# Block products with shared sums for an FFN's down projection

## The chip, the cores and the metric

One core of one Trainium2 chip. The metric is the device time of one execution in microseconds; for the kernel before it is the median of three runs. A profile of one execution stands beside it.

## The reference

An encoder layer for 1024 tokens of width 1024, all in float32:

```python
x = layer_norm(a * x + 0.5 * swiglu(x, ffn1...), ln1...)
x = layer_norm(a * x + hybrid_mixer(x, ...), ln2...)
x = layer_norm(a * x + 0.5 * swiglu(x, ffn2...), ln3...)

def swiglu(x, w_gate, w_up, w_down):
    return (silu(x @ w_gate) * (x @ w_up)) @ w_down
```

`a` is 2^0.25, and the FFN width is 2816, that is 22 tiles of 128. The mixer is neighbourhood attention beside differential attention. The change touches only `@ w_down` of the two FFNs and what makes its operands.

## The kernel before, in words

TensorE multiplies in the type fp32r. To hold accuracy, every float32 operand is split in two: `hi`, a cast of the value on ACT (line 65), and `lo`, the value less `hi`, on DVE or POOL (line 66). A product is then three matmuls, hi x hi, hi x lo and lo x hi, summed in PSUM (`mm3`, lines 79 to 81). `split_w` (line 68) is load, cast and subtraction in one; its load goes through one of two staging buffers, `wst`.

Stages follow each other in time: gate/up of FFN1 (to about 430 us), its down product and normalisation (to about 715), the mixer, gate/up of FFN2 (1336 to 1762), its down product and the last normalisation.

**Gate/up** (`gate_up`, line 179) makes, for each of the 22 FFN tiles `f`, the 128 x 1024 tile h = 0.5 silu(gate) * up and stores it in DRAM (`hTd`, lines 195 to 210). Tiles 0 and 1 take plain products. Tiles 2 to 21 take a product of 2 x 2 blocks (gate and up by two halves of the model width; the same halves by two halves of the tokens) by seven block products in place of eight: sums of blocks of x are made once (`S2`, `S3`, `S4`), sums of blocks of the weights for each tile, in a tile `wr` of seven slots (`sums`, lines 238 to 240), and `splits` (line 245) then splits the seven. One turn of the loop at line 302 is seven products of 12 matmuls each. `wr` has one buffer: the load for the next tile (line 217) can start when the last split of this one has read it. `finish(f)` multiplies and stores. In the last turns `split_w` also fetches the first operands of the down product.

**Down** (`down_phase`, line 340) computes y[token block] += h[f] x w_down[f]. It walks over `CHUNKS`: eight pairs of FFN tiles, two single tiles, and a last chunk of four. For each chunk and each of eight token blocks `Rows.down` (line 114) sums the chunk's matmuls in a PSUM bank for either half of the 1024 columns, and DVE adds the bank to the float32 row block y in SBUF (line 127; the first chunk is copied by ACT, line 125). Operands of the chunk ahead are fetched by `split_w` with the subtraction on POOL. The residual is loaded into `xp` and added on the way (lines 356 to 363). In the last chunk each finished row block is normalised.

Engines run in order, each its own queue; all these DMAs are issued by SP (SyncE). The order within a queue is that of a planner, which takes instructions by their place in the program and by when it reckons their inputs to be there, and so moves them past each other: in the loop, the load for the next tile goes out ahead of the store of the tile before.

PSUM has eight banks: pool `psA` has two buffers of two banks, `psB` four of one.

Of the kernel before, what the change touches and what calls it, by code (L numbers as in the profile page):

```python
# [9 lines left out]
FT = mybir.dt.float32  # L10
FR = mybir.dt.float32r
# [3 lines left out]
OP = mybir.AluOpType  # L15
AX = mybir.AxisListType
TAIL = 3
# [3 lines left out]
P = 128  # L21
S = 1024
DM = 1024
# [21 lines left out]
def tile_hybrid_layer(ctx: ExitStack, tc: tile.TileContext, I: dict, out: bass.AP, dbg=None):  # L45
# [51 lines left out]
    hTd = [dr.tile([NF, P, S], FT, name=f"hTd{i}") for i in range(2)]  # L97
# [80 lines left out]

    def gate_up(n, wgu, wd, W0=None, prelude=None):


        with ExitStack() as es:
# [12 lines left out]
            def finish(f):  # L195
                h = wst.tile([P, 1024], FT, name="wst")
                V.scalar_tensor_tensor(h, u.rearrange("p t c -> p (t c)"), 0.5, sg.rearrange("p t c -> p (t c)"),
                                       OP.mult, OP.mult)
                dma(hTd[n][f], h)

            def plain(f, wt, ts):
                for t in ts:
                    h = tb_.tile([P, 512], FT, name="t")
                    ps = psA.tile([P, 2, 512], FT, name="psA")
                    for j in range(2):
                        mm3(ps[:, j], [wt(j, k) + xk(t, k) for k in range(KT)])
                        flush()
                    A.activation(sg[:, t], ps[:, 0], AF.Silu)
                    V.scalar_tensor_tensor(h, ps[:, 1], 0.5, sg[:, t], OP.mult, OP.mult)
                    dma(hTd[n][f, :, t * 512:(t + 1) * 512], h)  # L210
# [22 lines left out]
            def sums(f):  # L233
                l = L[f]
                o = wa.tile([P, 2, 512], FR, name="wa")
                split(o[:, 0], o[:, 1], l[:, 4], V)
                O[f, 4] = o[:, 0], o[:, 1]
                V.tensor_tensor(l[:, 0:4:3], l[:, 2:4], l[:, 3:5], OP.subtract)  # L238
                V.tensor_tensor(l[:, 5], l[:, 0], l[:, 4], OP.add)  # L239
                V.tensor_tensor(l[:, 6], l[:, 1], l[:, 5], OP.subtract)  # L240

            def splits(f, part):
                a, b = ((1, 5), (0, 3), (2, 6))[part]
                o = wb.tile([P, 2, 2, 512], FR, name="wb")
# [43 lines left out]
            wb = es.enter_context(tc.tile_pool(name=f"wb{n}", bufs=4))  # L288
            for i in range(3):
                splits(2, i)  # L290
            plain(1, at(1), (0,))

# [9 lines left out]
            for f in range(2, NF):  # L302
# [5 lines left out]
                prod(b, f, 1, A12)  # L308
                V.tensor_tensor(sg[:, 0], B[f, 1], b, OP.add)
# [5 lines left out]
                if more:  # L315
                    sums(f + 1)
                prod(a, f, 0, S3, False)
# [3 lines left out]
                if more:  # L321
                    splits(f + 1, 0)
                    first(f + 1)
                    splits(f + 1, 1)
                prod(a, f, 6, A22, False)
# [6 lines left out]

                k = f - (NF - 6)
                if 0 <= k < 4:
                    down0.append(split_w((hTd[n], wd)[k % 2][k // 2]))
        return down0

    CHUNKS = [(f, f + 1) for f in range(0, NF - 6, 2)] + [(NF - 6,), (NF - 5,), tuple(range(NF - 4, NF))]

    def down_phase(es, n, wd, down0, resid, g, b, post):  # L340

        m = Rows(es, n)
        hp = es.enter_context(tc.tile_pool(name=f"hp{n}", bufs=4))
        wp = es.enter_context(tc.tile_pool(name=f"wp{n}", bufs=4))
        xp = es.enter_context(tc.tile_pool(name=f"xp{n}", bufs=2))
        m.small(es, n)
        Hs, Ws = {0: down0[0], 1: down0[2]}, {0: down0[1], 1: down0[3]}

        def fetch(f):
            Hs[f] = split_w(hTd[n][f], *(() if f == NF - 1 else (hp, "hd")))  # L350
            Ws[f] = split_w(wd[f], *(() if f == NF - 1 else (wp, "wd")))

        def part(f):
            return lambda tb: (Hs[f][:, 0, tb * P:(tb + 1) * P], Hs[f][:, 1, tb * P:(tb + 1) * P])

        def residual(tb):
            x = xp.tile([P, DM], FT, name="xp")
            dma(x, resid(tb))

            def add():  # L360
                V.scalar_tensor_tensor(m.y[tb], x, ALPHA, m.y[tb], OP.mult, OP.add)
            return add

        for f in CHUNKS[1]:
            fetch(f)
        add = None
        for i, fs in enumerate(CHUNKS):
            last = i == len(CHUNKS) - 1
            ahead = [f for c in CHUNKS[i + 1:i + 2] if i for f in c]

            def each(tb):
                nonlocal add
                if 2 <= i < 6 and tb % 4 == 1:
                    add = residual(2 * (i - 2) + tb // 4)
                if add and tb % 4 == 3:
                    add()
                    add = None
                if tb % 2 == 0 and ahead:
                    fetch(ahead.pop(0))
                if i == 6 and tb == 7:  # L380
                    m.load_gb(g, b)

            m.down([part(f) for f in fs], [Ws[f] for f in fs], None if i == 0 else 1.0,
                   (lambda tb, st: post(m, tb, st)) if last else None, each)
            for f in ahead:
                fetch(f)
# [546 lines left out]
```

## Time and profile before

| | us |
|---|---|
| runs of the kernel before | 2022.59, 2018.19, 2023.49 |
| median | 2022.59 |
| profiled execution | 2018.42 |
| its span, first to last instruction | 2016.6 |
| TensorE busy | 1972.8 |
| DVE, ACT, POOL busy | 1168.2, 720.9, 424.2 |

PE is TensorE's matmuls, PEld its weight loads, DVE is VectorE, ACT ScalarE, POOL GpSimd, SP the engine that issues the DMAs. Busy times are shares of one execution and overlap; matmuls are pipelined, so a matmul's own duration is longer than the distance from one to the next. "Idle before" is the time in which an engine stood still ahead of the instruction, with what ended it behind the arrow. Lines such as L127 are those of the kernel.

### The profile page before, as it was taken

The numbers are of one execution on the slowest core, as the hardware profiler recorded it, in microseconds if no ns is written. First come the engines' busy times: TensorE is split into PE (matmuls) and PEld (weight loads), VectorE is DVE, ScalarE is ACT, GpSimd is POOL, SyncE is SP. The second block draws the span as 40 slices with busy tenths as digits, with TensorE's granted clock in tenths as the row PEclk, the third lists the DMA queues.
The fourth block names the chain that finished last, engine by engine and source line by source line (L and its number), as shares of the span: only waits on it lengthen the run. The fifth ranks groups of instructions, "written<-read, shape, count | busy, mean of one in ns | idle before, by whom it ended". The sixth has DMA issues, their size and how long they took to land. (4 is left out here: it accounts for less than half of the span.)

```text
span 2016.6 us, 24187 instructions
## 1 busy us (share of the span) xinstructions
PE 1972.8 (98%) x9368; PEld 1602.4 (79%) x9368; DVE 1168.2 (58%) x1803; ACT 720.9 (36%) x1206; POOL 424.2 (21%) x276
## 2 busy tenths in 40 slices
PE   9999999999999999999999999999999999999998
PEld 7788888887887778888777777888888788877877
DVE  8445455534657856777663345885545446336667
ACT  5233333332122245656544454123333333231121
POOL 0000000105345221111044443100000001044355
PEclk9999999999999999999999999999999999999999
DMA  4212212224323231112122226122221223144332
GB/s 163 79 73 94 84 74 105 98 95 156 124 98 132 91 108 40 37 50 61 29 55 65 62 74 230 63 84 78 79 84 74 94 70 119 64 167 145 106 104 84
DMA packets 51891, 186.05 MB, mean 92 GB/s; under 512 B 7360, under 2 KB 11328, under 8 KB 46400
## 3 DMA queue, kind: packets, MB, share of 16 engines
q1 hardware_dynamic: 51776, 184.50, 27.0%
q8 instruction: 74, 1.21, 0.3%
q14 instruction: 41, 0.34, 0.1%
HBM read 136.24 MB, written 39.85 MB: 87 GB/s over the span
## 5 line engine op out<-in xcount | busy, mean ns | idle before, releaser
L127 DVE SCALAR_TENSOR_TENSOR y<-y,psB 128x512 f32<-128x512 f32 (+1 forms) x358 | 238.8, 676 | 201.1 <-PE psB L81 197.2
L66 POOL TENSOR_TENSOR wsp<-wst,wsp 128x1024 fp32r<-128x1024 f32 x40 | 97.9, 2449 | 945.5 <-ACT wsp L65 945.5
L79 PE MATMUL psB<-wd,hd 128*128 128x512 f32 (+1 forms) x620 | 241.6, 390 | 5.4 <-DVE y L127 4.0
L80 PE MATMUL psB<-wd,hd 128*128 128x512 f32 (+1 forms) x620 | 240.5, 388 | 3.9 <-POOL wd L66 3.9
L81 PE MATMUL psB<-wd,hd 128*128 128x512 f32 (+1 forms) x620 | 240.2, 387 | 0.0
L79 PE MATMUL psA<-s,wb 128*128 128x512 f32 x480 | 189.7, 395 | 0.0
L81 PE MATMUL psA<-s,wb 128*128 128x512 f32 x480 | 187.2, 390 | 0.0
L80 PE MATMUL psA<-s,wb 128*128 128x512 f32 x480 | 186.8, 389 | 0.0
L66 DVE TENSOR_TENSOR wb<-wr,wb 128x1024 fp32r<-128x1024 f32 x120 | 157.0, 1317 | 47.3 <-ACT wb L65 47.1
L480 PE MATMUL psB<-x,wsp 128*128 128x512 f32 x384 | 161.2, 420 | 0.0
L65 ACT CAST wb<-wr 128x1024 fp32r<-128x1024 f32 x120 | 125.0, 1051 | 96.9 <-DVE wr L239 87.0
L482 PE MATMUL psB<-x,wsp 128*128 128x512 f32 x384 | 152.7, 398 | 0.0
L481 PE MATMUL psB<-x,wsp 128*128 128x512 f32 x384 | 151.4, 394 | 0.0
L79 PEld LDWEIGHTS psB<-wd,hd 128*128 128x128 f32 x620 | 117.5, 189 | 31.4 <-DVE y L127 5.7
L66 POOL TENSOR_TENSOR hd<-wst,hd 128x1024 fp32r<-128x1024 f32 x38 | 91.3, 2403 | 240.5 <-ACT hd L65 240.5
L80 PEld LDWEIGHTS psB<-wd,hd 128*128 128x128 f32 x620 | 117.4, 189 | 27.9 <-POOL wd L66 4.5
L81 PEld LDWEIGHTS psB<-wd,hd 128*128 128x128 f32 x620 | 117.3, 189 | 23.4
L79 PE MATMUL psA<-x,wb 128*128 128x512 f32 x320 | 129.1, 404 | 1.5 <-ACT t L313 1.2
L238 DVE TENSOR_TENSOR wr<-wr 128x1024 f32<-128x1024 f32 x40 | 48.9, 1223 | 134.5 <-DMA wr<-in_wgu 134.5
L65 ACT CAST hd<-wst 128x1024 fp32r<-128x1024 f32 x38 | 40.0, 1052 | 240.8 <-PE psB L81 159.8
L80 PE MATMUL psA<-x,wb 128*128 128x512 f32 x320 | 125.2, 391 | 0.0
L81 PE MATMUL psA<-x,wb 128*128 128x512 f32 x320 | 125.0, 391 | 0.0
(171 smaller groups left out, 4019.9 us busy)
## 6 DMA issues: line engine op xcount, KB each, us to landing
wr<-in_wgu SPq DMA_DIRECT2D x42, 1024.0 KB, 4.8
wst<-hTd SPq DMA_DIRECT2D x44, 512.0 KB, 3.2
wst<-in_wd SPq DMA_DIRECT2D x44, 512.0 KB, 3.5
hTd<-wst SPq DMA_DIRECT2D x40, 512.0 KB, 2.6
wst<-in_w_in SPq DMA_DIRECT2D x24, 512.0 KB, 3.5
Q<-Q SPq DMA_DIRECT2D x32, 256.0 KB, 2.9
xp<-in_x SPq DMA_DIRECT2D x8, 512.0 KB, 4.4
x1d<-y SPq DMA_DIRECT2D x8, 512.0 KB, 2.9
```

What stands on the lines that cost most here:

```text
L65: A.copy(hi, x)
L66: eng.tensor_tensor(lo, x, hi.bitcast(FT), OP.subtract)
L79: T.matmul(ps, ah, bh, start=start and j == 0, stop=False, skip_group_check=skip)
L80: T.matmul(ps, ah, bl, start=False, stop=False, skip_group_check=skip)
L81: T.matmul(ps, al, bh, start=False, stop=j == n - 1, skip_group_check=skip)
L127: V.scalar_tensor_tensor(y[:, ds_], y[:, ds_], mode, ps, OP.mult, OP.add)
L238: V.tensor_tensor(l[:, 0:4:3], l[:, 2:4], l[:, 3:5], OP.subtract)
L480: T.matmul(ps, hi, xh, start=k == 0, stop=False)
L481: T.matmul(ps, hi, xl, start=False, stop=False)
L482: T.matmul(ps, lo, xh, start=False, stop=k == KT - 1)
```

## The change

FFN tiles 2 to 19 are taken as nine pairs. For a pair, the down product is one of 2 x 2 blocks: two tiles of h by two halves of the tokens, and the two tiles' rows of w_down by two halves of the columns. It is made by seven block products instead of eight. Each of the seven is summed over all nine pairs in PSUM (four banks, one for each of four token blocks) before anything is read. Four of the seven start from the sums that an earlier product left in its banks. Tiles 0, 1, 20 and 21 (`PLAIN`) stay plain; they are the last chunk, with the normalisation.

The operands are sums of blocks. Those of h are made in `finish`, in a tile of eight slots, seven of which go to DRAM once per pair (`hSd`). Those of w_down are made by `load_down` and `sum_down`, also in the gate/up loop, and four go to DRAM (`wTd`). `fetch_down` loads the two halves of an operand pair (128 x 512 of h, 128 x 512 of w) by a DMA each and splits them as one tile, with the subtraction on DVE. It is called four times in the last turn of the gate/up loop, and by `ahead` in the down stage, nine operands ahead of their use. Splits of the gate/up loop now use the pool `wsp` (four buffers), which they share with these operands, in place of `wb`. The residual is loaded into y itself at the start of the stage and scaled with the first add of each block.

```diff
-TAIL = 3
+NP = 9
+PLAIN = (0, 1, 20, 21)
...
-    hTd = [dr.tile([NF, P, S], FT, name=f"hTd{i}") for i in range(2)]
+
+    hPd = [dr.tile([4, P, S], FT, name=f"hPd{i}") for i in range(2)]
+    hSd = [[dr.tile([P, 7, 512], FT, name=f"hSd{i}_{p}") for p in range(NP)] for i in range(2)]
+    wTd = [[dr.tile([P, 4, 512], FT, name=f"wTd{i}_{p}") for p in range(NP)] for i in range(2)]
...
+    DOWN = [(0, (0, 0)), (1, (1, 0)), (4, 2), (3, 1), (5, 0), (6, (1, 1)), (2, 3)]
+
+    def fetch_down(n, wd, k, stage, pool, tag):
+
+        st = stage.tile([P, 1024], FT, name="wst")
+        if k < 7 * NP:
+            i, p = divmod(k, NP)
+            a, b = DOWN[i]
+            dma(st[:, 0:512], hSd[n][p][:, a])
+            dma(st[:, 512:1024], wd[2 + 2 * p + b[0], :, b[1] * 512:(b[1] + 1) * 512] if isinstance(b, tuple)
+                else wTd[n][p][:, b])
+        else:
+            j = (k - 7 * NP) // 2
+            dma(st, wd[PLAIN[j]] if k % 2 == 0 else hPd[n][j])
+        sp = pool.tile([P, 2, 1024], FR, name=tag)
+        split(sp[:, 0], sp[:, 1], st, V)
+        return sp
+
+    def sum4(l):
+
+        V.tensor_tensor(l[:, 0:4:3], l[:, 2:4], l[:, 3:5], OP.subtract)
+        V.tensor_tensor(l[:, 5], l[:, 0], l[:, 4], OP.add)
+        V.tensor_tensor(l[:, 6], l[:, 1], l[:, 5], OP.subtract)
+
...
             def finish(f):
-                h = wst.tile([P, 1024], FT, name="wst")
-                V.scalar_tensor_tensor(h, u.rearrange("p t c -> p (t c)"), 0.5, sg.rearrange("p t c -> p (t c)"),
-                                       OP.mult, OP.mult)
-                dma(hTd[n][f], h)
+                uu, ss = u, sg
+                if f in PLAIN:
+                    h = wst.tile([P, 1024], FT, name="wst")
+                    to = h.rearrange("p (t c) -> p t c", t=2)
+                else:
+                    p, o = divmod(f - 2, 2)
+                    if o == 0:
+                        H[0] = hs_.tile([P, 8, 512], FT, name="hs")
+                    h = H[0]
+                    to = h[:, 1:3] if o else h[:, 0:8:7]
+                V.scalar_tensor_tensor(to, uu, 0.5, ss, OP.mult, OP.mult)
+                if f in PLAIN:
+                    dma(hPd[n][PLAIN.index(f)], h)
+                elif o == 0:
+                    V.tensor_tensor(h[:, 5], h[:, 0], h[:, 7], OP.subtract)
+                else:
+                    V.tensor_tensor(h[:, 3], h[:, 7], h[:, 2], OP.add)
+                    V.tensor_tensor(h[:, 4], h[:, 3], h[:, 0], OP.subtract)
+                    V.tensor_tensor(h[:, 6], h[:, 1], h[:, 4], OP.subtract)
+                    dma(hSd[n][p], h[:, 0:7])
+
+            H = {}
+
+            def load_down(p):
+                l = H[1] = wt_.tile([P, 7, 512], FT, name="wt")
+                f = 2 + 2 * p
+                dma(l[:, 1:3], wd[f + 1].rearrange("p (b c) -> p b c", b=2))
+                dma(l[:, 4], wd[f, :, 0:512])
+                dma(l[:, 3], wd[f, :, 512:1024])
+
+            def sum_down(p):
+                l = H[1]
+                sum4(l)
+                dma(wTd[n][p][:, 0], l[:, 0])
+                dma(wTd[n][p][:, 1], l[:, 3])
+                dma(wTd[n][p][:, 2:4], l[:, 5:7])
 
...
-                    dma(hTd[n][f, :, t * 512:(t + 1) * 512], h)
+                    dma(hPd[n][f, :, t * 512:(t + 1) * 512], h)
...
-                V.tensor_tensor(l[:, 0:4:3], l[:, 2:4], l[:, 3:5], OP.subtract)
-                V.tensor_tensor(l[:, 5], l[:, 0], l[:, 4], OP.add)
-                V.tensor_tensor(l[:, 6], l[:, 1], l[:, 5], OP.subtract)
+                sum4(l)
...
-                o = wb.tile([P, 2, 2, 512], FR, name="wb")
+                o = wsp.tile([P, 2, 1024], FR, name="wsp").rearrange("p i (b c) -> p i b c", c=512)
...
-            wb = es.enter_context(tc.tile_pool(name=f"wb{n}", bufs=4))
-            for i in range(3):
-                splits(2, i)
+            hs_ = es.enter_context(tc.tile_pool(name=f"hs{n}", bufs=1))
+            wt_ = es.enter_context(tc.tile_pool(name=f"wt{n}", bufs=1))
+            splits(2, 0)
+            splits(2, 1)
             plain(1, at(1), (0,))
+            splits(2, 2)
+            load_down(0)
 
...
+                if not more:
+                    down0.append(fetch_down(n, wd, 0, wst, wsp, "wsp"))
...
                 finish(f)
-
-                k = f - (NF - 6)
-                if 0 <= k < 4:
-                    down0.append(split_w((hTd[n], wd)[k % 2][k // 2]))
+                p, o = divmod(f - 2, 2)
+                if o == 0 and p < NP:
+                    sum_down(p)
+                elif p + 1 < NP:
+                    load_down(p + 1)
+            down0.append(fetch_down(n, wd, 3, wst, wsp, "wsp"))
         return down0
 
-    CHUNKS = [(f, f + 1) for f in range(0, NF - 6, 2)] + [(NF - 6,), (NF - 5,), tuple(range(NF - 4, NF))]
...
-        hp = es.enter_context(tc.tile_pool(name=f"hp{n}", bufs=4))
-        wp = es.enter_context(tc.tile_pool(name=f"wp{n}", bufs=4))
-        xp = es.enter_context(tc.tile_pool(name=f"xp{n}", bufs=2))
+        hp = es.enter_context(tc.tile_pool(name=f"hp{n}", bufs=6))
+        sp_ = es.enter_context(tc.tile_pool(name=f"sp{n}", bufs=6))
...
+        ops = list(down0)
+        N = 7 * NP + 2 * len(PLAIN)
+
+        def ahead(k):
+            while len(ops) <= min(k, N - 1):
+                own = len(ops) % 10 < 4
+                ops.append(fetch_down(n, wd, len(ops), sp_, wsp if own else hp, "wsp" if own else "hd"))
+
+        def halves(t, c):
+            return [m.y[4 * t + T_][:, c * 512:(c + 1) * 512] for T_ in range(4)]
+
+        def product(i, banks, start):
+            for p in range(NP):
+                k = i * NP + p
+                ahead(k + 9)
+                o = ops[k]
+                for T_ in range(4):
+                    a = slice(T_ * P, (T_ + 1) * P)
+                    for j, (x, w) in enumerate(((0, 0), (0, 1), (1, 0))):
+                        T.matmul(banks[T_], o[:, x, a], o[:, w, 512:1024], start=start and p == 0 and j == 0,
+                                 stop=p == NP - 1 and j == 2, skip_group_check=not start)
+
+        def add(t, c, banks, mode=1.0):
+            for y, ps in zip(halves(t, c), banks):
+                V.scalar_tensor_tensor(y, y, mode, ps, OP.mult, OP.add)
+
+        def four():
+            return [psB.tile([P, 512], FT, name="psB") for _ in range(4)]
+
+        A_ = [psA.tile([P, 2, 512], FT, name="psA") for _ in range(2)]
+        A_ = [x[:, i] for x in A_ for i in range(2)]
+        ahead(6)
+        for tb in range(4):
+            dma(m.y[tb], resid(tb))
+        product(0, A_, True)
+        add(0, 0, A_, ALPHA)
+        B_ = four()
+        for tb in range(4, 8):
+            dma(m.y[tb], resid(tb))
+        product(1, B_, True)
+        add(0, 0, B_)
+        product(2, A_, False)
+        add(0, 1, A_, ALPHA)
+        C_ = four()
+        product(3, C_, True)
+        add(1, 1, C_, ALPHA)
+        product(4, A_, False)
+        add(1, 1, A_)
+        m.load_gb(g, b)
+        product(5, C_, False)
+        add(0, 1, C_)
+        product(6, A_, False)
+        add(1, 0, A_, ALPHA)
+        hw = ops[7 * NP:]
+
+        def part(h):
+            return lambda tb: (h[:, 0, tb * P:(tb + 1) * P], h[:, 1, tb * P:(tb + 1) * P])
+
+        m.down([part(h) for h in hw[0::2]], hw[1::2], 1.0, lambda tb, st: post(m, tb, st))
         return m
```

## Rows read from the trace of the kernel before

**Rows 1.** The page's first part: busy time, share of span, instructions.

```profile
PE 1972.8 (98%) x9368; PEld 1602.4 (79%) x9368; DVE 1168.2 (58%) x1803; ACT 720.9 (36%) x1206; POOL 424.2 (21%) x276
```

**Rows 2.** Timeline, first down stretch: start us, length us, engine, line, operation.

```profile
503.54 0.39 PE L80 MATMUL psB<-wd,hd 128*128 128x512 f32 x1
...
507.62 0.39 PE L80 MATMUL psB<-wd,hd 128*128 128x512 f32 x1
```

**Rows 3.** Busy time by stretch, columns named in the first line.

```profile
core 0: us, PE busy (x) PEld busy (x) DVE busy (x) ACT busy (x) POOL busy (x), PEclk, DMA share, GB/s
48.00:430.00 382.00, 380.52 (x1654) 306.61 (x1653) 195.22 (x214) 129.15 (x182) 9.66 (x4) 1.00 0.23 85
430.00:670.00 240.00, 228.53 (x996) 186.56 (x995) 130.37 (x179) 55.75 (x65) 105.59 (x44) 0.99 0.36 122
1382.00:1762.00 380.00, 379.95 (x1652) 306.16 (x1651) 188.32 (x207) 124.32 (x177) 9.76 (x4) 1.00 0.22 82
1762.00:2016.60 254.60, 239.30 (x1064) 197.02 (x1062) 151.92 (x216) 57.61 (x63) 126.83 (x55) 0.99 0.36 122
```

**Rows 4.** TensorE's waits, whole span: total us, times, longest us.

```profile
PE psB L79 <- DVE y L127: 4.0, 4, 1.4
PE psB L80 <- POOL wd L66: 3.9, 2, 1.9
PE psB L80 <- POOL wsp L66: 3.8, 2, 1.9
...
PE psB L79 <- ACT wd L65: 1.4, 2, 0.9
...
PE psB L79 <- ACT wsp L65: 0.5, 2, 0.3
```

**Rows 5.** Groups: line, operation, shapes, count, busy us, mean ns, idle before.

```profile
L127 DVE SCALAR_TENSOR_TENSOR y<-y,psB 128x512 f32<-128x512 f32 x346 | 234.0, 685 | 198.5 <-PE psB L81 194.6 <-DMA y<-x1d 3.8
...
L66 DVE TENSOR_TENSOR wb<-wr,wb 128x1024 fp32r<-128x1024 f32 x120 | 157.0, 1317 | 47.3 <-ACT wb L65 47.1 <-PE psA L81 0.3
...
L66 POOL TENSOR_TENSOR wd<-wst,wd 128x1024 fp32r<-128x1024 f32 x38 | 96.6, 2543 | 24.7 <-ACT wd L65 24.1
...
L238 DVE TENSOR_TENSOR wr<-wr 128x1024 f32<-128x1024 f32 x40 | 48.9, 1223 | 134.5 <-DMA wr<-in_wgu 134.5
...
L65 ACT CAST hd<-wst 128x1024 fp32r<-128x1024 f32 x38 | 40.0, 1052 | 240.8 <-PE psB L81 159.8 <-DMA wst<-hTd 71.2 <-POOL wd L66 9.8
...
L239 DVE TENSOR_TENSOR wr<-wr 128x512 f32<-128x512 f32 x40 | 27.3, 683 | 0.0
```

**Rows 6.** DMA issues: count, KB each, median us to landing.

```profile
wr<-in_wgu SPq DMA_DIRECT2D x42, 1024.0 KB, 4.8
...
wst<-in_wd SPq DMA_DIRECT2D x44, 512.0 KB, 3.5
...
wst<-in_wgu SPq DMA_DIRECT2D x4, 256.0 KB, 3.1
```

**Rows 7.** Busy time in 10 us of loads, columns as in rows 3.

```profile
1240.00:1250.00 10.00, 10.00 (x46) 8.29 (x45) 7.74 (x12) 3.75 (x6) 2.40 (x1) 1.00 0.81 306
```

**Rows 8.** Timeline of one gate/up turn, FFN1, columns as in rows 2.

```profile
329.65 0.69 DVE L330 TENSOR_TENSOR u<-t,psA 128x512 f32<-128x512 f32 x1 [4.92 <-PE psA L81]
...
340.17 0.69 DVE L320 TENSOR_TENSOR u<-t,psA 128x512 f32<-128x512 f32 x1 [2.28 <-ACT t L319]
...
341.12 1.23 DVE L66 TENSOR_TENSOR wb<-wr,wb 128x1024 fp32r<-128x1024 f32 x1 [0.26 <-ACT wb L65]
...
342.37 0.33 SPq L217 DMA_DIRECT2D wr<-in_wgu  x1
...
347.15 1.23 DVE L238 TENSOR_TENSOR wr<-wr 128x1024 f32<-128x1024 f32 x1 [4.81 <-DMA wr<-in_wgu]
```

**Rows 9.** TensorE's waits, 48 to 430 us.

```profile
PE psA L79 <- ACT t L313: 1.2, 1, 1.2
PE psA L79 <- DVE u L320: 0.2, 1, 0.2
```

More of the change, by code (lines that the diff above doesn't have):

```diff
@@ L316, in gate_up @@
                     sums(f + 1)
+                else:
+                    down0.append(fetch_down(n, wd, 1, wst, wsp, "wsp"))
                 prod(a, f, 0, S3, False)
@@ L324, in gate_up @@
                     splits(f + 1, 1)
+                else:
+                    down0.append(fetch_down(n, wd, 2, wst, wsp, "wsp"))
                 prod(a, f, 6, A22, False)
@@ L340, in down_phase @@
     def down_phase(es, n, wd, down0, resid, g, b, post):
         m = Rows(es, n)
-        hp = es.enter_context(tc.tile_pool(name=f"hp{n}", bufs=4))
-        wp = es.enter_context(tc.tile_pool(name=f"wp{n}", bufs=4))
-        xp = es.enter_context(tc.tile_pool(name=f"xp{n}", bufs=2))
+        hp = es.enter_context(tc.tile_pool(name=f"hp{n}", bufs=6))
+        sp_ = es.enter_context(tc.tile_pool(name=f"sp{n}", bufs=6))
         m.small(es, n)
-        Hs, Ws = {0: down0[0], 1: down0[2]}, {0: down0[1], 1: down0[3]}
@@ L349, in fetch @@
[L349 to L386, printed above, removed]
+        ops = list(down0)
```

## The prediction

> **What bounds the kernel now.** I read the page's first part, then busy time by stage, then TensorE's waits, then the DVE, ACT and DMA rows of the two places that the change touches. TensorE is busy 1972.8 of 2016.6 us [rows 1], but busy time of pipelined matmuls says little, so I took the pace: 18 matmuls of 512 columns start in 507.62 - 503.54 = 4.08 us, 0.2267 us each [rows 2]. Weight loads hide under that pace. In gate/up TensorE has 380.5 busy of 382 us and 379.95 of 380: that loop waits for nothing. In the down stretches it has 228.5 of 240 and 239.3 of 254.6 us [rows 3]: matmul count sets most of these, and a remainder is waits. So the kernel is bound by the number of matmuls nearly throughout; DVE is half idle in both stages (195 of 382, 130 of 240 us).
>
> **Removed: matmuls.** Before, 18 FFN tiles take 18 x 8 token blocks x 2 column halves x 3 = 864 matmuls per FFN. After, 7 products x 9 pairs x 4 token blocks x 3 = 756. The other four tiles keep 4 x 48 = 192. So 108 go per FFN, 216 in all: 216 x 0.2267 = **-49.0 us**, all on the path.
>
> **Removed: waits in the down stretches.** TensorE waited 4.0 us for the y adds, 3.9 + 3.8 us for POOL's split of an operand and 1.4 + 0.5 us for ACT's [rows 4]; together 13.6 us, both FFNs. The POOL half of a split costs about 2.5 us [rows 5], and only two staging buffers feed it. The new fetch puts it on DVE, where a subtraction of this shape takes 1.2 to 1.3 us [rows 5], has six staging buffers and runs nine operands ahead of use. An operand serves 12 matmuls, 12 x 0.2267 = 2.72 us; it needs ACT 1.05 and DVE 1.3 us. What is late next? DVE over one down stretch: 71 splits x 1.3 = 92 and 28 + 16 y adds x 0.68 = 30, so 122 of about 215 us, beside a normalisation that stays as it was. ACT: 71 x 1.05 = 75 us. The y adds fall from some 160 to 44, and in the products each product's four banks are wanted again a whole product (9 x 2.72 = 24.5 us) later. Neither engine is next to bind; I take **-12** of the 13.6. Bounds: 0 and -13.6. TensorE's granted clock is 0.99 in both down stretches and 1.00 in gate/up [rows 3]: some of the time after a wait ran at 1.2 instead of 2.4 GHz. (1 - 0.99) x 494.6 us = up to 5 us lost; part of it lies beside the tail, so **-2**, bounds 0 and -5.
>
> **Moved: the operand transfers.** 63 of 71 operands now come as two 256 KB loads, where 44 came as one of 512 KB. A tile wants 0.524 MB per 2.72 us = 193 GB/s; with the eight residual tiles (4.2 MB) in the first two products (49 us) some 278 GB/s. Before, a 256 KB load lands in 3.1 us, one of 512 KB in 3.5 [rows 6], and with several under way the engines moved 306 GB/s at a busy share of 0.81 in a 10 us stretch [rows 7]. SP issues one in 0.33 us. With six staging buffers and 3.1 + 1.05 + 1.3 + waiting, some 7 us around, a buffer supplies an operand every 1.2 us, under 2.72. Price 0 while this overlaps. The ends: operand 4 to 9 write into memory that the gate/up loop holds to its last product, so their casts start there; four operands are ready or nearly (10.9 us of matmuls), and a split each 1.3 us keeps ahead. The last operand of the plain tiles takes the buffer of operand 60, two products of 2.72 us before it is wanted, against 1.05 + 1.3. I take **+3** for both FFNs' edges; bounds 0 and +10 (the 3.9 + 3.8 + 2 us of such edges now).
>
> The Trainium skill speaks against this part: "DMA: Bandwidth & Descriptors", section "Bandwidth", asks for transfers of at least 1 MiB to reach 75% of peak, and its table has 138 GB/s at 64 KB and 341 at 1 MB. Were 256 KB loads held to the lower figure, an operand would take 3.8 us, an estimate from that page, and the down stage 63 x 2 x 1.08 = 136 us more. The trace has single transfers no faster than that (256 KB in 3.1 us), but several at once at 306 GB/s, so I follow the row.
>
> **Added in gate/up: sums and stores.** For each pair of tiles DVE gets, beside the old multiply: one 512-column subtraction at the even tile (0.68), three at the odd (2.05), and the weight sums, 1.22 + 0.68 + 0.68 = 2.59 [rows 5]. That is 5.32 us per pair, 18 pairs in all: 95.8 us. Bounds: 0 where DVE would have idled, +95.8 if all of it held TensorE up. Where does it land? In one turn of the loop, from the u add at 329.65 on, DVE is busy for eight us, then idles 2.3 us before the u add at 340.17 and 4.8 us before the next load lands at 347.15 [rows 8]: about 7 us of 19 idle, 2.66 us wanted on average. What sits behind is a ring: the last split (341.12) frees the weight tile, its reload is issued at 342.37, lands 4.8 us later [rows 6, 8], and the next turn's sums wait for it. Before that split DVE does 9.0 us of work in 11.5: six instructions of 512 columns at 0.68 and four of 1024 at 1.22. With 3.27 us more (even tile) it needs 12.3, so the ring slips 0.8 us; with 2.05 (odd) it fits. 18 slips of 0.8 us are 14 us if TensorE's order has no other work there. It has: seven products a turn, of which only one (4 x 3 matmuls) needs the first fresh operand; today's waits in that loop of FFN1 are 1.2 + 0.2 us [rows 9]. I take **+6**.
>
> DMA traffic per pair rises by the sum tile of 1.8 MB (for two stores of 0.5), 1 MB of down weights read and 1 MB of sums written, 2.8 MB in 38 us; at 306 GB/s that is 9 us, beside 2 MB of gate/up weights. If a weight reload queues behind 1 MB of it, it lands some 3 us late: the stored sums wait for DVE on SP's queue, and the next reload can stand behind that store. The reload is issued when its tile falls free, at about 13 us in the turn, and the stores after the boundary, so I put it at 0 and leave 3 us x 18 = 54 in the bounds. The weight sums wait for their load on DVE; u add, multiply and next splits stand behind it, but that load has a turn's head start. The operands 0 to 3 fetched in the last turn lie where DVE has no next tile to split: 0.
>
> **Sum.** 2018.42 (span 2016.6 and 1.8 around it) - 49.0 - 12 - 2 + 3 + 6 = 1964.4. The profiled execution lies 4.2 below the median of the runs shown, 2022.59; adding that gives **1968 us**, 2.7% less.
>
> **Rivals.**
> *A, the forecast* (0.67): TensorE's work falls by 49 us and the operand waits mostly go. 1952 (all waits gone, nothing new: 2022.6 - 49 - 13.6 - 5 = 1955, and 3 of spread) to 1985.
> *B, the loop gives back part* (0.20): the ring slips every turn and TensorE waits 0.5 to 1.2 us in each of 40 turns, 20 to 48 us. 1985 to 2010. For it: DVE is solid for eight us after each boundary. Against: the waits of that loop are 1.4 us now.
> *C, the other side: DVE's new sums become the loop's path* (0.08). Place: the boundary of each turn, where the sums stand ahead of the next tile's own sums and splits. Price 95.8 us in full: 2022.6 - 49 - 14 + 96 = 2056. It turns slower once 63 us, two thirds of the 95.8 (1.6 us a turn), is on the path. For it: in-order queues, one sum tile and one weight tile without a second buffer. Against: 7 idle us a turn.
> *D, the operand feed binds the down stage* (0.05): if loads of halves cost 3.1 us each with little overlap, a tile takes more than 2.72 us; at 3.3 us, 126 tiles x 0.6 = 73 us, so 2022.6 - 49 + 73 = 2047. The break-even is 0.39 us a tile. Against: 306 GB/s with several under way [rows 7]. The Trainium skill's table, above, is this rival at another price (136 us, some 2110); its chance is held in D's.
>
> **Numbers.** 0.3% of 2022 is about 6 us, what a measurement here can tell from no change. Faster holds A and B: 0.87. C and D end mostly slower, 0.09, and what of B to D comes out near even is 0.04. The range leaves out about 2 in 10: from A's lower end, 1952, to 2002, most of B; A's own range is 1952 to 1985.
>
> **What would show it.** Matmuls down from 9368 by 216, down stretches some 30 us shorter each, with no wait for POOL; gate/up stretches of 380 to 385 us. Wrong if a gate/up stretch grows by over 25 us, with TensorE waiting for DVE's splits or the reload landing late (B, C); or if down matmuls wait for the split of a fetched operand, landing times above 6 us (D).

## The result, and the profile after

The changed kernel takes 1967.02 us (median of four runs, 1965.29 to 1969.43) against 2020.39 for the kernel before in the same comparison: 0.9737 of its time, 95% interval 0.9716 to 0.9757. The forecast was 1968. Its profiled execution took 1969.43 us with a span of 1967.7; before, 2018.42 and 2016.6.

The page's first part of the changed kernel, and rows of its DMA issues (count, KB each, median us to landing):

```profile
PE 1926.4 (98%) x9152; PEld 1562.2 (79%) x9152; DVE 1217.6 (62%) x1823; ACT 762.3 (39%) x1228; POOL 208.8 (11%) x188
...
wst<-hSd SPq DMA_DIRECT2D x126, 256.0 KB, 3.6
wst<-wTd SPq DMA_DIRECT2D x72, 256.0 KB, 3.7
wst<-in_wd SPq DMA_DIRECT2D x54, 256.0 KB, 4.8
```

Matmuls fall from 9368 to 9152 [rows 1], the 216 of the forecast. POOL gives up half its busy time and DVE has 49 us more.

Busy time by stretch of the changed kernel, columns as in [rows 3]; the two short ones lie at the starts of the down stages:

```profile
48.00:430.00 382.00, 378.14 (x1637) 303.60 (x1636) 228.16 (x275) 123.35 (x174) 0.00 (x0) 1.00 0.41 151
449.00:691.00 242.00, 236.06 (x1075) 195.85 (x1074) 153.41 (x184) 85.59 (x89) 21.38 (x12) 0.98 0.57 191
456.00:466.00 10.00, 8.21 (x23) 6.25 (x24) 6.92 (x7) 5.24 (x6) 0.00 (x0) 0.66 1.02 389
1340.00:1720.00 380.00, 376.28 (x1630) 301.60 (x1629) 228.76 (x274) 122.11 (x175) 0.00 (x0) 1.00 0.41 149
1742.00:1967.70 225.70, 214.65 (x960) 177.25 (x958) 137.04 (x160) 79.24 (x75) 28.52 (x15) 0.98 0.56 189
1748.00:1758.00 10.00, 7.40 (x25) 5.49 (x26) 6.78 (x7) 5.08 (x6) 0.00 (x0) 0.83 1.03 387
```

TensorE now idles 3.9 of 382 and 3.7 of 380 us in gate/up (1.5 and 0.05 before), and 5.9 + 11.1 us in the down stages where it was 11.5 + 15.3 [rows 3]. TensorE's waits over the whole span, the first five:

```profile
PE psA L435 <- ACT wsp L66: 7.5, 3, 3.1
PE psA L80 <- ACT t L377: 5.3, 9, 0.9
PE psA L818 <- DVE st L822: 4.8, 2, 2.9
PE psA L161 <- DVE y L153: 3.1, 1, 3.1
PE psA L80 <- DVE u L386: 2.2, 3, 1.2
```

All rows of [rows 4] are gone, those for POOL among them. In their place stand three waits for a cast of an operand (L435 is a down matmul), of 2.9, 1.6 and 3.1 us, which end at 457.8, 1727.3 and 1750.6 us, and in gate/up twelve short ones, for the PSUM copy at L377 and the u add at L386. The rows at L818 and L161 belong to the mixer and to a normalisation.

By stage, in the profiled execution of each kernel (us). A gate/up stage ends with its last u add, FFN1's down stage with the last row block's transposes:

| | gate/up 1 | down 1 | mixer | gate/up 2 | down 2 to the end |
|---|---|---|---|---|---|
| before | 444.2 | 270.5 | 617.7 | 429.4 | 254.8 |
| after | 449.6 | 241.2 | 615.7 | 435.4 | 225.8 |
| e2_edge | 448.1 | 235.1 | 616.1 | 432.9 | 220.6 |
| e3_pool_split | 447.3 | 243.0 | 618.1 | 436.7 | 227.8 |
| e4_two_stage | 447.4 | 268.5 | 616.9 | 432.6 | 261.4 |
| e5_quarter_loads | 446.9 | 237.5 | 618.6 | 433.7 | 224.5 |
| e8_before_fewer | 443.3 | 242.2 | 619.0 | 429.7 | 226.7 |
| e9_no_wstream | 444.2 | 244.0 | 620.0 | 431.8 | 225.5 |
| e10_no_hsums | 443.8 | 239.5 | 619.0 | 435.6 | 225.3 |
| e12_paced | 448.2 | 240.4 | 618.6 | 434.2 | 224.1 |

The down stages give 29.3 and 29.0 us. The mixer, which no kernel touches, spreads over 4 us here, so a stage of a single execution says little under that. Four kernels have the changed gate/up loop as it is, e5 with the loads of its last turn cut in two (after, e3, e4, e5): their two gate/up stages sum to 882.4 us on average (880.0 to 885.0); before and e8, with the old loop, to 873.3. The loop's price is thus some **9 us** (6 to 12).

### The profile page after: what moved, and what is told of

Same layout as the page of the kernel before. It is cut to its first block, busy times and chain, and to the rows that moved or that the text cites. A ratio compares the mean times of both kernels' runs of the same rounds, so it can differ in the third digit from the quotient of the medians.

```text
span 1967.7 us, 24088 instructions
## 1 busy us (share of the span) xinstructions
PE 1926.4 (98%) x9152; PEld 1562.2 (79%) x9152; DVE 1217.6 (62%) x1823; ACT 762.3 (39%) x1228; POOL 208.8 (11%) x188
## 4 chain that ended last, share of the span: by engine, by line
PE 42%; DMA 3%; DVE 3%; ACT 1%; issue 1%; POOL 0%; SPq 0%; POOLq 0%; DVEq 0%; ACTq 0%
PE psA L80 5%; PE psA L82 5%; PE psA L81 5%; PE psA L435 5%; PE psB L435 4%; PE psB L80 3%; PE psB L81 3%; PE psB L82 3%; PE psB L568 2%; PE psB L570 2%; PE psB L569 2%; PE psB L851 2%; PE psA L818 1%; DMA wr<-in_wgu 1%; PE psB L843 1%
## 5 line engine op out<-in xcount | busy, mean ns | idle before, releaser
L80 PE MATMUL psA<-x,wsp 128*128 128x512 f32 x448 | 181.5, 405 | 8.8 <-ACT t L377 5.3
L80 PE MATMUL psA<-s,wsp 128*128 128x512 f32 x480 | 189.6, 395 | 0.0
L82 PE MATMUL psA<-s,wsp 128*128 128x512 f32 x480 | 187.4, 390 | 0.0
L81 PE MATMUL psA<-s,wsp 128*128 128x512 f32 x480 | 186.7, 389 | 0.0
L66 ACT CAST wsp<-wr 128x1024 fp32r<-128x1024 f32 x124 | 128.9, 1049 | 128.9 <-DVE wr L205 121.3
L81 PE MATMUL psA<-x,wsp 128*128 128x512 f32 x448 | 175.8, 392 | 0.5 <-DVE x L67 0.5
L82 PE MATMUL psA<-x,wsp 128*128 128x512 f32 x448 | 175.1, 391 | 0.0
L67 DVE TENSOR_TENSOR wsp<-wr,wsp 128x1024 fp32r<-128x1024 f32 x124 | 149.5, 1223 | 12.9 <-ACT wsp L66 12.9
L67 DVE TENSOR_TENSOR hd<-wst,hd 128x1024 fp32r<-128x1024 f32 x84 | 102.0, 1223 | 73.0 <-ACT hd L66 68.2
L66 ACT CAST wsp<-wst 128x1024 fp32r<-128x1024 f32 (+1 forms) x90 | 93.0, 1034 | 105.5 <-DMA wst<-in_wd 27.9
L80 PEld LDWEIGHTS psA<-x,wsp 128*128 128x128 f32 x448 | 84.1, 188 | 45.4 <-ACT t L377 16.1
L435 PE MATMUL psA<-hd 128*128 128x512 f32 x504 | 116.2, 389 | 0.0
L435 PEld LDWEIGHTS psA<-hd 128*128 128x128 f32 x504 | 94.6, 188 | 19.7
L80 PEld LDWEIGHTS psA<-s,wsp 128*128 128x128 f32 x480 | 90.0, 188 | 25.4 <-ACT sg L394 8.2
```

Source lines behind the costliest of these rows:

```text
L66: A.copy(hi, x)
L67: eng.tensor_tensor(lo, x, hi.bitcast(FT), OP.subtract)
L80: T.matmul(ps, ah, bh, start=start and j == 0, stop=False, skip_group_check=skip)
L81: T.matmul(ps, ah, bl, start=False, stop=False, skip_group_check=skip)
L82: T.matmul(ps, al, bh, start=False, stop=j == n - 1, skip_group_check=skip)
L435: T.matmul(banks[T_], o[:, x, a], o[:, w, 512:1024], start=start and p == 0 and j == 0, stop=p == NP - 1 and j == 2, skip_group_check=not ...
```

## The experiments

**Matmuls alone (e8_before_fewer).** The kernel before, with less TensorE work and nothing else:

```diff
-            T.matmul(ps, ah, bl, start=False, stop=False, skip_group_check=skip)
+            T.matmul(ps, ah, bl, start=False, stop=j == n - 1 and j in two, skip_group_check=skip)
+            if j in two:
+                continue
```

> The kernel before, with 112 matmuls per FFN left out of the down product and nothing else changed: the third partial product (lo x hi) of FFN tiles 2 to 8 is not computed. Theory: the down stage is on the path matmul by matmul, 224 x 0.2267 = 50.8 us less, 0.975 of the kernel before (0.971 to 0.979). Rival: the old operand feed (two staging buffers, POOL) is nearly the bound by itself and holds these tiles once their matmuls are fewer: a fall of 25 us or less, 0.988 or above.

1962.78 us, 0.973 (0.9711 to 0.9749). That is 224 matmuls for 51 to 58 us by the interval; 224 x 0.2267 = 50.8 is its lower end. The profiles show what lies above it: TensorE's idle time in the two down stages falls from 26.8 to 21.6 us. The matmul term needs nothing but the pace, and fewer matmuls alone took some 5 us of the old waits along.

**The edge (e2_edge).** What happens at 450 us in the changed kernel, by its timeline (start, length, engine, line; L449 loads the residual):

```profile
449.49 0.33 SPq L449 DMA_DIRECT2D y<-in_x  x1
...
450.00 0.33 SPq L192 DMA_DIRECT2D wst<-hSd  x1
450.30 1.23 DVE L235 SCALAR_TENSOR_TENSOR wst<-u,sg 128x1024 f32<-128x1024 f32 x1
...
451.55 0.33 SPq L237 DMA_DIRECT2D hPd<-wst  x1
451.68 4.84 ACT L66 CAST hd<-wst 128x1024 fp32r<-128x1024 f32 x5 [5.30 <-DVE wst L235]
451.93 0.42 SPq L193 DMA_DIRECT2D wst<-in_wd  x1
...
456.69 1.04 ACT L66 CAST wsp<-wst 128x1024 fp32r<-128x1024 f32 x1 [0.18 <-DMA wst<-in_wd]
...
457.79 1.22 PE L435 MATMUL psA<-wsp 128*128 128x512 f32 x2 [2.87 <-ACT wsp L66]
```

The fourth operand is fetched by the loop's last turn, through the loop's staging buffers. The first half of its load leaves at 450.00, behind the residual's first load, which held SP for 9.4 us until TensorE's last gate/up matmuls were done. The second half stands on SP behind the store of the last h tile, which waits for DVE's multiply, and leaves at 451.93. ACT meanwhile casts five operands of the down stage, which are wanted later. These casts are not what is late: when they are done, ACT stands 0.18 us more for the load, which ends the wait, and takes the fourth operand at 456.69. TensorE stands 2.87 us. At 1744 to 1750.6 us the same costs 3.1, and there ACT stands 0.66 us for the load. Behind each wait the granted clock is at its lower level, 1.2 GHz, for part of the next stretch: it is 0.66 and 0.83 in the 10 us rows above, by which I estimate (1 - 0.66) x 10 + (1 - 0.83) x 10 = 5.1 us. So the two edges cost 6.0 + 5.1 = 11 us, beside the third wait, in FFN2's last gate/up turn, where again the second half of an operand's load stands behind an h store (issued at 1723.55 and 1723.91). The experiment leaves the fourth operand to the down stage's own staging:

```diff
-            down0.append(fetch_down(n, wd, 3, wst, wsp, "wsp"))
         return down0
```

> The changed kernel with one operand (the fourth) fetched at the start of the down stage through its own staging buffers instead of in the last gate/up turn through the shared pair, so that its cast stands ahead of five others on ACT. Theory: TensorE's wait of 2.9 and 3.1 us at the start of the two down stages, and the half clock after it (0.66 and 0.83 over 10 us, worth 3.4 and 1.7 us), go: about 10 us less, 1957 us (1954 to 1960). Rival: the DMA engines are full there (a share of 1.02, 389 GB/s), so the operand lands no earlier and the wait stays or moves to the next operand: 1967 us, within 3.

1956.39 us, 0.9702 (0.9683 to 0.9721), about 7 us under the changed kernel by the ratios. The two kernels ran in different comparisons and the intervals still touch; below, e12_paced and e13_edge_paced differ in this edit alone and ran on one chip: 1969.05 against 1956.48, 12.6 us, with no run of the one among those of the other. By stage, the profiles of e2_edge and the changed kernel have 6.1 + 5.2 = 11.3 us between them in the down stages. Busy time at the same two places, in this kernel:

```profile
456.00:466.00 10.00, 10.00 (x46) 8.26 (x45) 6.21 (x6) 5.27 (x5) 0.00 (x0) 1.00 1.04 390
...
1742.00:1752.00 10.00, 10.00 (x46) 8.29 (x45) 7.02 (x6) 6.93 (x7) 0.00 (x0) 1.00 1.05 392
```

TensorE is solid and its clock full, while the DMA engines move as much as before (390 GB/s). The operand's load has left SP by 437.14 here, 10.9 us ahead of the residual's, and its cast starts at 448.05. The place of the load on SP made the wait, not the traffic on the DMA engines; that the operand now has a staging buffer of its own is part of the same edit. This kernel beats both.

**Staging depth (e4_two_stage), splitting engine (e3_pool_split), load size (e5_quarter_loads).** One line each:

```diff
# e4_two_stage: staging of the down stage
-tc.tile_pool(name=f"sp{n}", bufs=6)
+tc.tile_pool(name=f"sp{n}", bufs=2)
# e3_pool_split: the subtraction on POOL but for the first four operands
-        split(sp[:, 0], sp[:, 1], st, V)
+        split(sp[:, 0], sp[:, 1], st, G if k > 3 else V)
# e5_quarter_loads: the h half so, and the w half alike
-            dma(st[:, 0:512], hSd[n][p][:, a])
+            for o in (0, 256):
+                dma(st[:, o:o + 256], hSd[n][p][:, a, o:o + 256])
```

> The changed kernel with two staging buffers in the down stage instead of six. Theory: a buffer goes round in about 3.6 (load) + 1.05 (ACT) + 1.25 (DVE) + 0.7 us = 6.6 us, so two give an operand every 3.3 us, above the 2.72 us of its matmuls: 0.6 x 126 = 75 us more, 2042 us (2010 to 2060), slower than the kernel before. Rival: the lead of nine operands covers it and the stage stays paced by TensorE: 1967 to 1975 us.

2033.27 us, 1.0081 (1.0059 to 1.0103): slower than the kernel before. Busy time in its first down stage, and its largest waits there:

```profile
430.00:660.00 230.00, 211.27 (x856) 158.19 (x854) 107.12 (x104) 77.75 (x77) 0.10 (x1) 0.99 0.58 188
```

```profile
PE psB L80 <- ACT hd L66: 5.5, 3, 2.4
PE psB L435 <- DVE wsp L67: 2.3, 5, 0.8
PE psA L435 <- DVE wsp L67: 2.1, 5, 0.8
```

With two buffers a load leaves only when a split two operands back is done, and TensorE waits at many operands, for either engine. The idle 18.7 us are only part of it: at the pace, 856 matmuls are 194 us, so the 211.27 busy us hide some 17 more. With this one count wrong, the change loses its whole gain.

> The changed kernel with the subtraction of the down operands on POOL, as before the change, for all but the first four of each stage. Theory: about 2.5 us on POOL against 2.72 us of matmuls for an operand leaves no room to catch up, so waits for POOL return at the start of each stage and now and then later: 1980 us (1973 to 1990). Rival: the six staging buffers and the lead of nine operands are what removed the waits, the engine does not matter: 1967 us, within 3. A third outcome, POOL above 2.72 us beside a busy DVE, would give 2.8 us x 126 or more, over 1985.

1971.71 us, 0.9774 (0.9751 to 0.9796): between the two theories, some 7 us above the changed kernel by the ratios, whose intervals touch; the profile's down stages show 3.8. POOL is busy 170.9 of 230 us (430 to 660) and keeps up. The engine is the small part of the waits' removal, the staging the large one.

> The changed kernel with each 256 KB load of the down stage cut into two of 128 KB (252 more loads, 1 KB rows). Theory: with six staging buffers loads overlap and SP issues four in 1.6 us of an operand's 2.72 us, so the stage stays paced by TensorE; only its crowded start gets a little worse: ratio 0.975 (0.973 to 0.979). Rival: small transfers starve the stage: with the rate falling in proportion an operand takes over 2.72 us, ratio 1.0 or more.

1962.48 us, 0.9729 (0.9711 to 0.9747): no cost that can be told. Its DMA issues:

```profile
wst<-hSd SPq DMA_DIRECT2D x252, 128.0 KB, 3.3
wst<-wTd SPq DMA_DIRECT2D x144, 128.0 KB, 3.4
wst<-in_wd SPq DMA_DIRECT2D x108, 128.0 KB, 3.1
```

Twice the transfers of half the size land in about the same time each (3.6, 3.7 and 4.8 us for 256 KB, above).

**What costs 9 us in gate/up.** My first theory was DVE's time for the sums. A turn at 101 us of the changed kernel, DVE, ACT and the matmul that waits:

```profile
100.98 0.69 DVE L67 TENSOR_TENSOR wa<-wr,wa 128x512 fp32r<-128x512 f32 x1 [0.58 <-ACT wa L66]
...
101.59 0.68 DVE L241 TENSOR_TENSOR hs<-hs 128x512 f32<-128x512 f32 x1
...
102.19 0.68 DVE L373 TENSOR_TENSOR sg<-t,psB 128x512 f32<-128x512 f32 x1
...
102.91 0.63 ACT L374 ACTIVATE sg<-sg 128x512 f32<-128x512 f32 x1 [1.96 <-DVE sg L373]
...
103.45 0.57 ACT L377 COPY t<-psA 128x512 f32<-128x512 f32 x1
104.07 0.50 PE L80 MATMUL psA<-x,wsp 128*128 128x512 f32 x1 [0.50 <-ACT t L377]
```

An h sum (L241) stands ahead of the add that Silu waits for; Silu stands on ACT ahead of the copy that frees a PSUM bank; TensorE wants that bank 0.50 us before the copy is done. But the waits are not spread over the turns. TensorE's busy time in stretches of 76 us, changed kernel:

```profile
48.00:124.00 76.00, 73.53 (x317) 58.40 (x316) 48.87 (x58) 23.23 (x33) 0.00 (x0) 1.00 0.58 208
124.00:200.00 76.00, 74.82 (x325) 60.17 (x324) 50.03 (x63) 24.39 (x34) 0.00 (x0) 1.00 0.58 214
200.00:276.00 76.00, 75.89 (x330) 61.12 (x330) 44.61 (x55) 25.61 (x36) 0.00 (x0) 1.00 0.31 118
```

The last two stretches idle 0.10 and 0.00. The waits fall where DMA traffic is double: the planner runs all nine weight tiles as fast as their one buffer comes free, one a turn, and the nine sets of stores to `wTd` go out from 55.1 to 207.6 us. In these turns both sets of sums stand on DVE. Six kernels looked for the cost; the edits:

```diff
# e1_no_sums: fills by POOL in place of both sets of sums
-                    V.tensor_tensor(h[:, 5], h[:, 0], h[:, 7], OP.subtract)
...
-                sum4(l)
+                G.memset(l[:, 0], 0.0)
+                G.memset(l[:, 5:7], 0.0)
# e9_no_wstream: no loads, sums and stores of the weights in the loop;
# the down stage reads plain halves of the weights in place of the four sums
...
-                if o == 0 and p < NP:
-                    sum_down(p)
-                elif p + 1 < NP:
-                    load_down(p + 1)
# e10_no_hsums: no sums of h, their slots hold zeros written once
...
-                    V.tensor_tensor(h[:, 3], h[:, 7], h[:, 2], OP.add)
...
# e12_paced: the weight load of a pair waits for an h tile
+                if p:
+                    G.tensor_copy(l[:, 1:5, 0:1], H[0][:, 0:4, 0:1])
# e13_edge_paced: e2_edge and e12_paced
# e15_edge_paced_first: e13, and the first pair's load in the loop's first turn
# e11_edge_hpool: e2_edge, and the sums of h on POOL
-                    V.tensor_tensor(h[:, 3], h[:, 7], h[:, 2], OP.add)
+                    G.tensor_tensor(h[:, 3], h[:, 7], h[:, 2], OP.add)
...
```

> The changed kernel with the operand sums left out of the gate/up loop: the sum slots of h and of the down weights are filled with zeros by POOL instead (so the sums are not computed); loads, stores and the down stage are as they were. Theory: the sums cost the loop about 6 us in all, through DVE (a late sg add, so a late Silu and PSUM copy on ACT), so 1961 us (1957 to 1964), and TensorE's waits in either gate/up stretch fall from 3.7 to about 1 us. Rival: the 6 us come from the added DMA traffic, which is unchanged here: 1967 us, within 2.

1974.2 us, 0.9795 (0.9769 to 0.9821), slower than the changed kernel, which neither theory had; its gate/up stages are 891.6 us. With no sums in its way the weight stream ran further ahead into the reloads of `wr`: from 48 to 124 us the DMA engines move 248 GB/s, where the changed kernel has 208. SP and DVE in this kernel:

```profile
93.98 0.33 SPq L247 DMA_DIRECT2D wt<-in_wd  x1
94.36 0.43 SPq L248 DMA_DIRECT2D wt<-in_wd  x1
95.22 0.33 SPq L249 DMA_DIRECT2D wt<-in_wd  x1
97.33 0.33 SPq L275 DMA_DIRECT2D wr<-in_wgu  x1
```

```profile
105.87 1.23 DVE L204 TENSOR_TENSOR wr<-wr 128x1024 f32<-128x1024 f32 x1 [2.46 <-DMA wr<-in_wgu]
```

The reload behind three weight loads takes 8.5 us (4.8 in [rows 6]), and TensorE idles 5.85 us between 48 and 124 us, then 1.25, then nothing. So taking the sums away also moved the transfers, and the run says nothing on DVE's time by itself.

> The changed kernel without the stream of down weights through the gate/up loop: no loads, sums (2.59 us of DVE per pair) or stores of them; the down stage reads plain halves of the weights in place of the four sums, so these sums are not computed. The sums of h stay. Theory: the weight sums lie mostly in DVE's gaps and the sums of h at the turn's boundary cost most of the 6 us, so 2 to 3 us less than the changed kernel: ratio to the kernel before 0.972 (0.971 to 0.9735). Rival: the weight stream's transfers beside the tile reload are what costs: 6 us or more less, 0.971 or below.

> The changed kernel without the sums of h: the summed slots of one lasting tile are zeros, written once, so four subtractions per pair (2.73 us of DVE) are not computed; its store and the whole weight stream stay. Theory: these sums stand at the turn's boundary ahead of the sg add, and taking them out gives back 3 to 5 us: ratio 0.9715 (0.970 to 0.9725). Rival: the weight stream costs, not these: 0.9735, no change. Third: that a freer DVE lets the weight stream run ahead and collide with the reloads, as where all sums were left out: 0.976 or more.

1963.69 us, 0.9736 (0.9717 to 0.9756), and 1963.91 us, 0.9738 (0.9718 to 0.9757): neither can be told from the changed kernel. The profiles do show gate/up shorter: 876.0 us for the two stages in e9 and 879.4 in e10, against 882.4. Gate/up of FFN1 in e9:

```profile
48.00:430.00 382.00, 381.09 (x1652) 306.02 (x1650) 209.59 (x251) 124.86 (x177) 0.00 (x0) 1.00 0.28 105
```

0.9 us idle where the changed kernel has 3.9; e10 has 0.8 there as well, with the weight stream at full pace beside it. In FFN1 either set of sums alone is hidden.

> The changed kernel with the weight tiles of pairs 2 to 9 tied to their place in the loop: POOL copies one column of the finished h tile into each block that the weight load then overwrites, so a load can't start before its turn. In the changed kernel's trace the planner runs all nine weight tiles in the first 160 us of a gate/up stretch, one a turn instead of one in two, and TensorE's idle time lies there (2.5, 1.2, then 0.1, 0.1 and 0.0 us in five stretches of 76 us). Theory: the bunched weight stream is what costs, by reloads of the gate/up weights that queue behind it and by DVE waiting for a weight load with the u add behind; tied down, 5 to 8 us come back: ratio 0.970 (0.969 to 0.972). Rival: the sums' DVE time itself costs, wherever they stand: 0.9735, no change.

1969.05 us, 0.9753 (0.9733 to 0.9773), no gain; its gate/up stages are 882.4 us, the average of the unpaced ones. TensorE's waits for the PSUM copy are 5.7 us in 13 places instead of 5.3 in 9, and in FFN1 it idles 0.9, 0, 0.2, 0.2 and 1.0 us in the five stretches of 76 us. The weight stream's place isn't what costs, and the theory falls. Its rival, DVE's time wherever it stands, fits but isn't shown: e9 took the weight stream's transfers away together with its sums.

> The tied weight stream together with the fourth operand fetched through the down stage's own staging buffers. Theory: the two gains lie in different stretches and add: 0.9665 (0.965 to 0.9685). Rival: one of them was noise, or they share a cause: 0.970 or above.

> As the one before, with the first pair's weight load tied too: it waits for the reload of the gate/up weights in the first turn instead of standing ahead of it. Theory: the first turns of both gate/up stretches lose 2 and 4 us in the changed kernel, and the tied first load gives back some 2 us more: 0.9655 (0.964 to 0.9675). Rival: tying the other pairs already removed it: no change from the one before.

1956.48 us, 0.9694 (0.9675 to 0.9713), and 1958.77 us, 0.9702 (0.9684 to 0.9721): no better than e2_edge. Against e12_paced, on the same chip, e13 shows the edge's worth once more: 12.6 us.

> The fourth operand as in e2_edge, and the sums of h on POOL in place of DVE; the weight stream as in the changed kernel. Theory: the sums of h are not what costs (from 200 us on, where they stand alone, TensorE idles 0.2 us in 228), so no gain on e2_edge's 0.970 (0.969 to 0.972). Rival: they hold the sg add up in every turn: 0.968 or below.

1980.82 us, 0.9823 (0.9802 to 0.9845): 24 us slower than e2_edge by the ratios. DVE's groups from 48 to 430 us in e2_edge, then in this kernel (count, busy us, mean ns), then one of POOL's:

```profile
L67 DVE TENSOR_TENSOR wsp<-wr,wsp 128x1024 fp32r<-128x1024 f32 x60 | 72.3, 1222 | 6.6 <-ACT wsp L66 6.6
...
L206 DVE TENSOR_TENSOR wr<-wr 128x512 f32<-128x512 f32 x19 | 13.0, 686 | 0.0
```

```profile
L67 DVE TENSOR_TENSOR wsp<-wr,wsp 128x1024 fp32r<-128x1024 f32 x60 | 83.1, 1402 | 8.6 <-ACT wsp L66 8.6
...
L206 DVE TENSOR_TENSOR wr<-wr 128x512 f32<-128x512 f32 x19 | 22.3, 1174 | 0.2
...
L386 DVE TENSOR_TENSOR u<-t,psA 128x512 f32<-128x512 f32 x19 | 13.1, 688 | 35.3 <-ACT t L385 35.3
```

```profile
L243 POOL TENSOR_TENSOR hs<-hs 128x512 f32<-128x512 f32 x9 | 18.3, 2036 | 0.7
```

DVE is relieved of 36 sums of 0.68 us a loop, and is still busier: 235.7 of 380 us from 48 to 428, against 227.7. While POOL works beside it, the splits grow by 10.8 us and these sums by 9.3. The gate/up stages take 903.3 us.

## Why the prediction was right, and where its terms were off

The forecast of the profiled execution was 1964.4 us, 54 less than before; it took 1969.43, 49.0 less. The terms against what the two profiles show:

| | forecast | measured |
|---|---|---|
| matmuls, by their count and the pace | -49.0 | -49.0 |
| waits of the down stages | -12 | -15.8 |
| clock, without the edges | -2 | -2.5 |
| edges, with their clock | +3 | +11.1 |
| gate/up | +6 | +11.4 |
| mixer | 0 | -2.0 |
| not accounted for | | -2.1 |

- **Matmuls, -49.0.** Right: 216 fewer, and e8 shows that this many are worth their pace in full without any other part of the change.
- **Waits, -12.** Right. TensorE's idle time in the down stages went from 26.8 to 17.0 us, with 6.0 of the 17.0 at the new edges: 15.8 of old waits are gone. That the six buffers carry this, as the prediction said, e4 shows; the lead of nine operands was not changed by itself. That POOL's speed mattered as well is the lesser part (e3). ACT and DVE did not become late: no wait for a split is left in the products.
- **Clock, -2.** Right by itself, and outweighed by the edges. (1 - granted clock) x length, summed over stretches of 10 us in the down stages, was 6.6 us before and is 9.2 after, of which the two edge rows are 5.1; in e2_edge it is 3.1 in all.
- **Edges, +3.** Mis-sized: 6.0 us of waits and 5.1 of clock, just beyond the upper bound of +10. The step that failed: "four operands are ready or nearly". The prediction looked at operands 4 to 9 and the memory that they write into; late was the fourth itself, whose load stood on SP behind the residual's first load and a store. What it queues behind was never asked. e2_edge removes both waits and their clock.
- **Gate/up, +6.** Right in kind, undersized: 11.4 us between the two profiles (1.6 of it the operand wait at 1727), 9 by the averages over kernels with either loop. TensorE's idle time grew by 8.4 of the 11.4, from 4.5 to 12.9 us; the other 3.0 are longer busy time, and no row shows why. The place was right too (DVE's turn is too full at times, and TensorE waits for the u add, or for the copy behind Silu). Wrong was how the sums are spread: the prediction put them at 5.32 us a pair, two turns, where in the loop's first half a weight tile's sums stand in every turn, because the planner empties that stream as early as it can. So was "that load has a turn's head start": in FFN2's first turn DVE waits 4.02 us for it, the u add behind it starts at 1363.30, and TensorE stands 1.24 us:

```profile
1362.15 1.23 DVE L204 TENSOR_TENSOR wt<-wt 128x1024 f32<-128x1024 f32 x1 [4.02 <-DMA wt<-in_wd]
...
1363.30 0.68 DVE L386 TENSOR_TENSOR u<-t,psA 128x512 f32<-128x512 f32 x1
...
1364.03 0.50 PE L80 MATMUL psA<-x,wsp 128*128 128x512 f32 x1 [1.24 <-DVE u L386]
```

- **Operand transfers, 0.** Right. The whole of rival D fails: operands land in 3.6 to 4.8 us by the median, under the 6 that were to show it, and e5's halves cost nothing. From 450 to 465 us, beside the residual's loads, single ones take up to 7.7 us in the changed kernel; in e2_edge they take up to 8.2 from 448 to 470 us, and no matmul waits for them there, so the six buffers cover that too. The Trainium skill, "DMA: Bandwidth & Descriptors", section "Bandwidth", wants 1 MiB or more a transfer; here 256 KB transfers and the residual's of 512 KB move 390 GB/s together, and operand loads of 128 KB leave the time where it was. The measurement decides: with several transfers in flight the size of one did not set the time of this stage.
- **Rivals B and C.** The loop gives back 9 us, not the 20 to 48 of B or the 63 of C's turning point.

The total came out closer than its terms: two costs were 13.5 us too low together, and 3.8 us more of old waits, 2 of the mixer's scatter and 2 unaccounted for made up for 8 of it. That 1968 lies within 1 us of the median is luck in part: the profiled execution missed its forecast by 5.0 us, but the 4.2 us added for the step from profile to median were not there, since the changed kernel's profile lies 2.4 us above its median. Set against 2020.39, the median of before in the final comparison, and not against 2022.59, the forecast would have been 2 us lower.

What stays open: e9 and e10 have gate/up stages 3 to 6 us shorter in the profile but time no faster, on the chip where e5, with the unchanged loop, took 1962.48. A profile is one execution, the intervals are 4 us to either side, and e9's first down stage was 2.8 us longer than the changed kernel's. Which part of the 9 us belongs to either set of sums isn't settled; only that moving the weight stream in time (e12) and moving sums to POOL (e11) don't win it back.

## What to carry to other kernels

Price a stage by its matmul count times the pace, then look at its first few operands one by one: which queue each load and each cast stands in, and what is ahead of it there; a wait of 3 us at such an edge cost nearly twice that here, by the half-speed stretch behind it. That isn't a rule: in e5 a wait of 2.6 us at the first edge left the granted clock at 1.00. Look also at when a stream of work with one buffer and no deadline is run: this planner ran it as early as the buffer allowed, so its work fell on half of the turns and not on the average one. Count staging buffers before engines: two instead of six turned a gain of 2.6% into a loss of 0.8%.

## What was not expected of the hardware

Instructions of DVE with two inputs in SBUF grew while POOL ran 128x512 sums of 1.7 to 2.0 us beside it: splits of 128x1024 from 1222 to 1402 ns on average, sums of 128x512 from 686 to 1174 (e11_edge_hpool against e2_edge), while the add that reads one input from PSUM stayed at 688. The averages hide two cases. A turn of e11_edge_hpool (start, length):

```profile
101.97 1.67 POOL L241 TENSOR_TENSOR hs<-hs 128x512 f32<-128x512 f32 x1 [19.09 <-DVE hs L235]
102.40 0.68 DVE L373 TENSOR_TENSOR sg<-t,psB 128x512 f32<-128x512 f32 x1
...
103.00 1.18 DVE L205 TENSOR_TENSOR wr<-wr 128x512 f32<-128x512 f32 x1
```

POOL's sum ends at 103.64. The DVE sum with two SBUF inputs starts before that and ends 0.55 us after it, not much less than the 0.69 us that it takes alone; the PSUM add inside the same stretch keeps its 0.68. Of the 60 splits, 50 kept 1220 ns, and the ten that started while a POOL sum ran took 2312. In e1_no_sums POOL only wrote its fills beside DVE (0.96 us for 128x1024), and the splits stayed at 1224 ns from 48 to 200 us, though five of the 24 had a fill beside them. The Trainium skill, "SBUF — State Buffer", section "SBUF: two separate sides", has this: VectorE and GpSimd lock a port pair against each other when the one has two SBUF inputs and the other reads SBUF. Both runs agree.

With a busy share of 1.02 to 1.05 the DMA engines moved 386 to 392 GB/s at the starts of the down stages; TensorE, ACT and DVE ran on in e2_edge without a wait there.
